# A hybrid attention and HGRN2 block on one core: the tensor engine's order written down in the source, with small products moved to common places

## The chip, the core and the metric

The program runs on one core of a Trainium2 chip. TensorE (PE) does the matrix products, VectorE (DVE) and ScalarE (ACT) the elementwise work, GpSimd (POOL) masks and powers, and SyncE (SP) issues the DMAs. Each engine works through its own list of instructions in order and stops at an instruction whose semaphores have not come. The metric is the device time of one execution, in microseconds (us).

## The reference

A block of a decoder for 512 positions of 1024 channels, in float32. One projection of the normalized input gives all branches; sliding-window attention with sinks and a gated linear recurrence (HGRN2) run in parallel, are merged by gates, and a SwiGLU layer follows.

```python
u = rmsnorm(h, norm_mix_g[layer])
p = jnp.einsum('bsd,de->bse', u, w_in[layer]) + b_in[layer]
aq, ak, av, hq, hf, hi, hg, gate_a, gate_b = split_columns(p)
y_attn = sliding_window_sink_attention(aq, ak, av, attn_sinks[layer])   # 16 heads, blocks of 128
y_hgrn = hgrn2_branch(hq, hf, hi, hg, lb_all[layer], hgrn_norm_g[layer]) # 8 heads, see below
ya = jnp.einsum('bse,ed->bsd', y_attn, w_branch_attn[layer])
yb = jnp.einsum('bse,ed->bsd', y_hgrn, w_branch_hgrn[layer])
merged = jax.nn.sigmoid(gate_a) * ya + jax.nn.sigmoid(gate_b) * yb
h = h + jnp.einsum('bsd,de->bse', merged, w_out[layer])
...
S_t = diag(f_t) S_{t-1} + k_t^T v_t ;  o_t = q_t S_t          # HGRN2, worked out in chunks
o = o * lax.rsqrt(jnp.mean(o * o, axis=-1, keepdims=True) + EPS)
o = o * norm_g * jax.nn.sigmoid(hg)
```

## The kernel before

**Large products.** Every float32 product of the projections is made of three products of split numbers (a high part and the rest, in fp32r). A projection (`project`, `mm3`, L404 to L406) is 24 matmuls of 128x512 into one PSUM tile `ps_big`; the values of HGRN (`values_hgrn`, L420 to L422) are 96 matmuls of 128x256 into `ps_v`. Weights come by DMA into `raw`; ACT makes the high part `wh` (L120) and DVE the rest `wl` (L126), two projections ahead, into three buffers each.

**The stream.** `stream()` is a generator that runs the projections in turn: queries and the gate of attention (`ga`), then for each of four pairs of heads `p` the HGRN values, then the projections `hf`, `hq` and `hg` for the two heads of the pair, and last the eight products `ya` with `w_branch_attn`. It yields three times in a projection (after a third, after two thirds and at the end) and six times in the values of a pair. Each yield is a slot.

**What stands beside it.** A table `beside` says after which slot each small step is called. An attention step `s` (group of four heads `s // 4`, block of queries `s % 4`) has three: `scores` (8 matmuls into `sc`, then the softmax on POOL, ACT and DVE, which ends with the multiplication of L507), `probs` (4 transposes into `pt`, L514; then ACT and DVE split the result and POOL masks it, L525 and L529) and `outputs` (2 or 4 matmuls into `pv`, L546). A head of HGRN has `hgrn_log` (ACT's Ln), `hgrn_prep` (a scan, exponentials and some thirteen operations on DVE, L629 to L658), `hgrn_intra` (matmuls into `pa` and `pc`), `hgrn_keys` (3 transposes `pk`), `hgrn_states` (`pu`), `hgrn_outputs` (matmuls into `po`, L705 and L707; then ACT squares them into `sq`, DVE sums, L713, and scales, L299, POOL takes the power, L300, and DVE writes the normalized `sq`, L715) and `hgrn_gate` (4 transposes of that `sq` into `pot`, L721, and DVE's product with the gate, L722). A pair's `hgrn_log` and `hgrn_prep` are called while the values of the next pair run (for the last pair: while the first `ya` runs).

**PSUM.** Small products share one tag of three buffers (`s1`); `sc` has a single buffer, and the large products have three.

**Who sets the order.** The program is recorded in the order of the calls, and a scheduler then places each engine's instructions by times that it estimates itself. So on PE the table only says about where a small product goes: the scheduler moves it behind further large products until its operands are due by the estimate. Later in the kernel, in the last part of the SwiGLU layer, a stretch is already under `tc.manual_schedule`, in which the named engines keep the order of the source.

Of the kernel before, what the change touches and what calls it, by code (L numbers as in the profile page):

```python
# [157 lines left out]
def block_kernel(ctx: ExitStack, tc: tile.TileContext, x, norm_mix_g, w_in, b_in,  # L158
# [153 lines left out]
    def transposed(half):  # L312
        xs = [ps1([P, 2, 256], "xs") for _ in range(3)] + [ps2([P, 4, 256], "xs")]
        views = [xs[j % 4][:, j // 4, :] for j in range(KD)]
        for t2 in range(2):
            t = 2 * half + t2
            if half == 0:
                normalize(t)
            for j in range(KD):
                pe.transpose(views[j][:, t2 * P:t2 * P + P], xt[:, t, j * P:(j + 1) * P],  # L320
                             ident)
        return views, xs[3][:, 2, 0:90]
# [19 lines left out]
    views, _ = transposed(0)  # L342
# [82 lines left out]
    def project(evac, ah=uh, al=ul):  # L425
        wh, wl = W.get()
        ps = psb([P, S], "ps_big")
        yield from mm3(ps, wh, wl, ah, al)
        evac(ps)
        yield  # L430
# [29 lines left out]
    def evac_q(c):  # L460
        def go(ps):
            bq = bias(c)
            for par in range(2):
                q = ap.tile([P, S], F32R, tag="q", bufs=8, name="qst")
                rs = slice(par * 64, par * 64 + 64)
                ot = slice(64 - par * 64, 128 - par * 64)
                act(q[rs], ps[rs], AF.Identity, bias=bq[rs])
                stt(q[ot], ps[rs], bq[rs], q.bitcast(F32)[rs], ALU.add, ALU.subtract)
                qsts[c // 64 + par] = q
        return go  # L470

    def evac_ga(j):
        def go(ps):
            act(m1[:, j, :], ps, AF.Identity, bias=bias(C_GA + P * j))
        return go
# [130 lines left out]
    def values_hgrn(p):  # L606
        wa, wb = W.get(), W.get()
        v = vals[p] = T("v", (P, NT, 256), 2, h1)
        for tp in range(2):
            ps = psb([P, 2, 256], "ps_v")  # L610
            for t2 in range(2):
                t = 2 * tp + t2
                mm3n(ps[:, t2, :], uh, ul, t, *wa, 0, True, False)
                yield
                mm3n(ps[:, t2, :], uh, ul, t, *wb, 4, False, True)
                tt(v[:, t, :], ps[:, t2, :], hib[:, 256 * p:256 * p + 256], ALU.add)
                if t2:
                    yield
# [107 lines left out]
    def evac_ya(j):  # L726
        def go(ps):
            tt(m1[:, j, :], ps, m1[:, j, :], ALU.mult)
        return go

    def stream():
        evac_q(0)(psq0)
        for i in range(4):
            for a in range(2):
                if i or a:
                    yield from project(evac_q(256 * i + P * a))
            if i:
                for a in range(2):
                    yield from project(evac_ga(2 * i - 2 + a))
        for a in range(2):  # L740
            yield from project(evac_ga(6 + a))
        for p in range(4):
            yield from values_hgrn(p)
            for ev in (evac_f, evac_hq, evac_hg):
                for a in range(2):
                    yield from project(ev(2 * p + a))
        for j in range(KD):
            yield from project(evac_ya(j), yh, yl)

    beside = {}  # L750

    def at(slot, f, *args):
        beside.setdefault(slot, []).append((f, args))
# [1 line left out]
    at(0, values)  # L755
    at(3, lower_bounds)
    for s in range(16):
        g0 = 3 * (1 + s)
        at(g0, scores, s // 4, s % 4)
        at(g0 + 4, probs, s // 4, s % 4)  # L760
        at(g0 + 8, outputs, s // 4, s % 4)
    at(3 * (1 + 15) + 8, open_hgrn)
    for p in range(4):
        g0 = 3 * (15 + 8 * p) + 24
        for a in range(2):
            hd = 2 * p + a
            at(g0, hgrn_log, hd)
            at(g0 + 2 * a + 1, hgrn_prep, hd)
            o = g0 + 8 + 9 * a
            for dt, f in ((0, hgrn_intra), (1, hgrn_keys), (3, hgrn_states),  # L770
                          (6, hgrn_outputs), (10, hgrn_gate)):
                at(o + dt, f, hd)
    slot = 0
    for _ in stream():
        for f, args in beside.pop(slot, ()):
            f(*args)
        slot += 1
    for s in sorted(beside):
        for f, args in beside[s]:
            f(*args)  # L780
    pools["h"].release()
    h1.release()
    h0.release()
# [227 lines left out]
    for kind, p in ffn[:-2]:  # L1011
# [5 lines left out]
        engines={mybir.EngineType.DVE, mybir.EngineType.Activation, mybir.EngineType.PE}))  # L1017
# [205 lines left out]
```

## Time and profile before

| | |
|---|---|
| median of 3 runs (lowest, highest) | 896.04 us (895.97, 896.45) |
| profiled execution | 895.81 us |
| its span, first to last instruction | 894.1 us |
| outside the span | 1.7 us |
| PE busy | 882.6 us, 99% of the span |
| DVE, ACT, POOL busy | 551.3, 397.0 and 155.1 us |
| the stretch that the change touches | about 31 to 425 us of the span |

In the rows of the profile, "L404 PE MATMUL ps_big<-uh,wh" is line 404, its engine and operation, and the tile written, an arrow and the tiles read; buffer numbers are left out. A row of the timeline has the start and the duration in us, and merges neighbours of one kind: x4 is four instructions as the chip ran them. A product of full float32 operands (`pa`, `pc`, `pu`, `po`) runs as two matmuls, so that its rows count double. Matmuls overlap: one of 128x512 is shown with 0.39 us, and the next starts 0.227 us after it.

### The profile page before, as it was taken

How to read it: one execution, taken by the hardware profiler on the slowest of the kernel's cores; microseconds unless marked ns; L12 is line 12 of the kernel's file. 1: busy time of each engine (PE TensorE's matmuls, PEld its weight loads, DVE VectorE, ACT ScalarE, POOL GpSimd, SP SyncE). 2: the span in 40 equal slices, each digit the busy share in tenths (PEclk: the TensorE clock that was granted, in tenths of full speed). 3: DMA queues.
4: the chain of work that ended last, by engine and by line, in shares of the span. 5: the costliest groups of instructions: out<-in, count | busy, mean ns of one | idle time of the engine just before them, and what ended most of it. 6: DMA issues, size and time to landing. Idle time of an engine off the chain costs nothing.

```text
span 894.1 us, 11244 instructions
## 1 busy us (share of the span) xinstructions
PE 882.6 (99%) x4410; PEld 746.8 (84%) x4410; DVE 551.3 (62%) x838; ACT 397.0 (44%) x637; POOL 155.1 (17%) x150
## 2 busy tenths in 40 slices
PE   8999999999999999999999999999999999999996
PEld 7988889888898988888888887888888888888785
DVE  5577877647494664844434345755655666566885
ACT  6566776646372544315223234332333333333454
POOL 3004434300000000000000002422133332122006
PEclk9999999999999999999999999999999999999999
DMA  8321211223213132221235232333343443435642
GB/s 261 95 95 48 95 48 48 95 95 95 95 28 114 48 115 74 94 81 62 94 96 189 93 95 89 107 134 113 122 141 96 141 127 108 135 101 174 252 163 95
DMA packets 74643, 97.26 MB, mean 109 GB/s; under 512 B 2043, under 2 KB 64605, under 8 KB 74589
## 3 DMA queue, kind: packets, MB, share of 16 engines
q1 hardware_dynamic: 74428, 96.27, 32.9%
q8 instruction: 35, 0.57, 0.3%
q10 hardware_dynamic: 160, 0.27, 0.1%
q14 instruction: 20, 0.16, 0.0%
HBM read 94.43 MB, written 2.10 MB: 108 GB/s over the span
## 4 chain that ended last, share of the span: by engine, by line
PE 96%; SPq 1%; DVE 1%; ACT 1%; POOL 0%; issue 0%; DMA 0%; DVEq 0%; POOLq 0%; ACTq 0%
PE ps_big L404 13%; PE ps_big L405 13%; PE ps_big L406 13%; PE ps_f L405 9%; PE ps_f L406 9%; PE ps_f L404 9%; PE s3y L989 3%; PE a22y L989 3%; PE s2y L989 3%; PE ps_v L421 2%; PE ps_v L422 2%; PE ps_v L420 2%; PE ps_o L421 2%; PE ps_o L422 2%; PE ps_o L420 2%; PE pv L546 1%
## 5 line engine op out<-in xcount | busy, mean ns | idle before, releaser
L120 ACT ACTIVATE wh<-raw 128x1024 fp32r<-128x1024 f32 (+1 forms) x168 | 172.3, 1031 | 344.4 <-PE ps_f L405 137.4
L126 DVE TENSOR_TENSOR wl<-raw,wh 128x1024 fp32r<-128x1024 f32 (+1 forms) x168 | 208.5, 1244 | 113.9 <-ACT wh L120 112.9
L404 PE MATMUL ps_big<-uh,wh 128*128 128x512 f32 x376 | 148.8, 396 | 0.0
L405 PE MATMUL ps_big<-ul,wh 128*128 128x512 f32 x376 | 147.8, 393 | 0.0
L406 PE MATMUL ps_big<-uh,wl 128*128 128x512 f32 x376 | 147.7, 393 | 0.0
L405 PE MATMUL ps_f<-u2l,wh 128*128 128x512 f32 x352 | 137.4, 390 | 0.0
L404 PE MATMUL ps_f<-u2h,wh 128*128 128x512 f32 x352 | 137.0, 390 | 0.2 <-ACT u2h L171 0.2
L406 PE MATMUL ps_f<-u2h,wl 128*128 128x512 f32 x352 | 137.0, 389 | 0.0
L406 PEld LDWEIGHTS ps_big<-uh,wl 128*128 128x128 f32 x376 | 70.7, 188 | 14.2
L405 PEld LDWEIGHTS ps_big<-ul,wh 128*128 128x128 f32 x376 | 70.8, 188 | 13.6
L404 PEld LDWEIGHTS ps_big<-uh,wh 128*128 128x128 f32 x376 | 70.7, 188 | 13.6
L405 PEld LDWEIGHTS ps_f<-u2l,wh 128*128 128x128 f32 x352 | 66.1, 188 | 14.0 <-issue 0.2
L404 PEld LDWEIGHTS ps_f<-u2h,wh 128*128 128x128 f32 x352 | 66.0, 188 | 14.0 <-ACT u2h L171 0.5
L406 PEld LDWEIGHTS ps_f<-u2h,wl 128*128 128x128 f32 x352 | 66.1, 188 | 13.9 <-issue 0.2
L954 POOL TENSOR_TENSOR zg<-zg,sgf 128x512 f32<-128x512 f32 x22 | 39.5, 1795 | 190.8 <-ACT sgf L176 190.8
L300 POOL TENSOR_TENSOR r<-ss,neghalf 128x4 f32<-128x4 f32 x8 | 10.1, 1262 | 232.8 <-DVE ss L299 232.8
L138 DVE TENSOR_TENSOR raw<-raw 128x512 f32<-128x512 f32 x44 | 31.7, 723 | 29.0 <-DMA raw<-in_w_ffn_down_dram 28.7
L951 DVE TENSOR_TENSOR zg<-ps_f,R 128x512 f32<-128x512 f32 x22 | 15.1, 691 | 38.0 <-PE ps_f L406 38.0
L955 POOL TENSOR_TENSOR zg<-zg,R 128x512 f32<-128x512 f32 x22 | 37.1, 1686 | 1.7
L420 PE MATMUL ps_v<-wh,uh 128*128 128x256 f32 x128 | 36.5, 285 | 0.0
L421 PE MATMUL ps_v<-wl,uh 128*128 128x256 f32 x128 | 36.3, 284 | 0.0
L422 PE MATMUL ps_v<-wh,ul 128*128 128x256 f32 x128 | 36.2, 284 | 0.0
(328 smaller groups left out, 1609.6 us busy)
## 6 DMA issues: line engine op xcount, KB each, us to landing
raw<-in_w_in_dram SPq DMA_DIRECT2D x27, 1024.0 KB, 5.2
raw<-in_w_ffn_gate_dram SPq DMA_DIRECT2D x11, 1024.0 KB, 5.2
raw<-in_w_ffn_up_dram SPq DMA_DIRECT2D x11, 1024.0 KB, 5.1
raw<-in_w_ffn_down_dram SPq DMA_DIRECT2D x11, 1024.0 KB, 4.8
raw<-in_w_ffn_down_dram SPq DMA_DIRECT2D x22, 512.0 KB, 4.5
raw<-in_w_branch_attn_dram SPq DMA_DIRECT2D x4, 1024.0 KB, 5.5
raw<-in_w_branch_hgrn_dram SPq DMA_DIRECT2D x4, 1024.0 KB, 4.8
raw<-in_w_out_dram SPq DMA_DIRECT2D x4, 1024.0 KB, 7.3
```

What stands on the lines that cost most here:

```text
L120: nc.scalar.activation(hv, src, AF.Copy)
L126: (low or nc.vector).tensor_tensor(lv, src, hv.bitcast(F32), ALU.subtract)
L138: add = lambda o, i0, i1: self.nc.vector.tensor_tensor(o, i0, i1, ALU.add)
L404: pe.matmul(ps, wh[:, k, :], ah[:, k, :], start=k == 0, stop=False)
L405: pe.matmul(ps, wh[:, k, :], al[:, k, :], start=False, stop=False)
L406: return raw_ins(pe.matmul(ps, wl[:, k, :], ah[:, k, :], start=False, stop=k == KD - 1))
L420: pe.matmul(ps, ah[:, k0 + k, ts], wh[:, k, :], start=first and k == 0, stop=False)
L421: pe.matmul(ps, ah[:, k0 + k, ts], wl[:, k, :], start=False, stop=False)
L422: pe.matmul(ps, al[:, k0 + k, ts], wh[:, k, :], start=False, stop=last and k == nk - 1)
L954: pool_e.tensor_tensor(zg, zg, sg, ALU.mult)
L955: pool_e.tensor_tensor(zg, zg, R, ALU.mult)
L989: pe.matmul(ps[i], x[:, ts], w, start=first and n == 0, stop=last and n == 2)
```

## The change

Three things change, all in the table and in the loop that works it off. First, the steps of attention move: `scores` of step s from slot 3 + 3s to slot 4 + 3s, `probs` from 4 to 6 slots behind `scores`, `outputs` from 8 to 12 slots behind. With these distances `outputs` of step s - 2, `probs` of step s and `scores` of step s + 2 fall on one slot. Second, in HGRN `hgrn_keys` moves from 1 slot behind `hgrn_intra` to the same slot, and `hgrn_gate` from 10 to 9 slots behind it, which for the first head of a pair is the slot of `hgrn_intra` and `hgrn_keys` of the second. Third, the loop runs under `tc.manual_schedule` for PE: PE keeps the order of the calls, while ACT, DVE, POOL and the DMAs are placed by the scheduler as before.

```diff
     for s in range(16):
-        g0 = 3 * (1 + s)
+        g0 = 4 + 3 * s
         at(g0, scores, s // 4, s % 4)
-        at(g0 + 4, probs, s // 4, s % 4)
-        at(g0 + 8, outputs, s // 4, s % 4)
-    at(3 * (1 + 15) + 8, open_hgrn)
+        at(g0 + 6, probs, s // 4, s % 4)
+        at(g0 + 12, outputs, s // 4, s % 4)
+    at(4 + 3 * 15 + 12, open_hgrn)
...
-            for dt, f in ((0, hgrn_intra), (1, hgrn_keys), (3, hgrn_states),
-                          (6, hgrn_outputs), (10, hgrn_gate)):
+            for dt, f in ((0, hgrn_intra), (0, hgrn_keys), (3, hgrn_states),
+                          (6, hgrn_outputs), (9, hgrn_gate)):
                 at(o + dt, f, hd)
     slot = 0
-    for _ in stream():
-        for f, args in beside.pop(slot, ()):
-            f(*args)
-        slot += 1
-    for s in sorted(beside):
-        for f, args in beside[s]:
-            f(*args)
+    with tc.manual_schedule(engines={mybir.EngineType.PE}):
+        for _ in stream():
+            for f, args in beside.pop(slot, ()):
+                f(*args)
+            slot += 1
+        for s in sorted(beside):
+            for f, args in beside[s]:
+                f(*args)
```

PE issues the same products before and after. Counted in its list from the first small product beside the stream to the last `hgrn_gate`, small products stand at 85 places between large ones before, and at 49 after. What follows is the order of instructions of the built programs; no time is in it.

The first place is on PE, in attention, where `ps_big` (projections) gives way to `ps_v` (the first HGRN values). Before:

```order
L489 MATMUL sc<-khh_430,qst 128x128
L490 MATMUL sc<-kll_432,qst 128x128
L405 MATMUL ps_big<-ul,wh_1370 128x512
...
L514 MATMUL pt<-ident,st 128x128 x4
L405 MATMUL ps_big<-ul,wh_1370 128x512
...
L420 MATMUL ps_v<-wh_1451,uh 128x256
L546 MATMUL pv<-ch,vhl_434 128x512
L421 MATMUL ps_v<-wl_1452,uh 128x256
L489 MATMUL sc<-khh_430,qst 128x256
L546 MATMUL pv<-cl,vhl_434 128x512
```

After:

```order
L406 MATMUL ps_big<-uh,wl_1337 128x512
L546 MATMUL pv<-ch,vhl_434 128x512
L546 MATMUL pv<-cl,vhl_434 128x512
...
L514 MATMUL pt<-ident,st 128x128 x4
L489 MATMUL sc<-khh_430,qst 128x256
L490 MATMUL sc<-kll_432,qst 128x256
...
L404 MATMUL ps_big<-uh,wh_1336 128x512
```

What stood at three places, partly mixed with large products, stands together: `pv` of one step, `pt` of a second and `sc` of a third.

The second place is on PE at the end of a pair's projections, where the second head's `po` is followed by the next values. Before:

```order
L406 MATMUL ps_big<-uh,wl_2375 128x512
L705 MATMUL po<-v,aT_1929 128x128 x2
L420 MATMUL ps_v<-wh_2419,uh 128x256
...
L707 MATMUL po<-st,lf 128x128
...
L422 MATMUL ps_v<-wh_2471,ul 128x256
L404 MATMUL ps_big<-uh,wh_2521 128x512
...
L420 MATMUL ps_v<-wh_2419,uh 128x256
...
L721 MATMUL pot<-ident,sq 128x128 x4
L420 MATMUL ps_v<-wh_2419,uh 128x256
```

After:

```order
L406 MATMUL ps_big<-uh,wl_2377 128x512
L705 MATMUL po<-v,aT_1988 128x128 x2
L707 MATMUL po<-st,lf 128x128
...
L420 MATMUL ps_v<-wh_2433,uh 128x256
...
L422 MATMUL ps_v<-wh_2473,ul 128x256
L721 MATMUL pot<-ident,sq 128x128 x4
L420 MATMUL ps_v<-wh_2433,uh 128x256
```

Between the end of `po` and `pot` stood 72 matmuls of `ps_v` (8 of them inside `po`) and 19 of `ps_big`; now 48 of `ps_v` stand there. The same holds at the end of the next pair. At the end of the third pair it was 73 of `ps_big` behind the last `po`, and is now 24.

The third place is on DVE at the same end of a pair: the operations of the next pair's `hgrn_prep`, among which the second head's sum (L713) and normalization (L715) stand. `E`, `K` and `QE` are tiles of `hgrn_prep`. Before:

```order
L629 SCALAR_TENSOR_TENSOR lf<-reset,lf 128x512 x2
L632 TENSOR_TENSOR d<-lf 128x512
L634 TENSOR_TENSOR e<-lf 128x512
L713 TENSOR_REDUCE ss_2513<-sq 128x4
...
L299 TENSOR_SCALAR ss_2513<-ss_2513 128x4
...
L656 TENSOR_TENSOR QE_2588<-q,lf 128x256
L616 TENSOR_TENSOR v<-ps_v,hib 128x256
L715 TENSOR_TENSOR sq<-po,r_2514 128x512
L646 TENSOR_TENSOR E_2632<-q,E_2632 128x512
```

After:

```order
L629 SCALAR_TENSOR_TENSOR lf<-reset,lf 128x512 x2
L632 TENSOR_TENSOR d<-lf 128x512
L634 TENSOR_TENSOR e<-lf 128x512
L713 TENSOR_REDUCE ss_2515<-sq 128x4
...
L299 TENSOR_SCALAR ss_2515<-ss_2515 128x4
...
L656 TENSOR_TENSOR QE_2590<-q,lf 128x256
L715 TENSOR_TENSOR sq<-po,r_2516 128x512
L646 TENSOR_TENSOR E_2634<-q,E_2634 128x512
```

DVE's list is the same down to L656; only one evacuation of values (L616) now stands behind L715 instead of before it. At the end of the third pair L715 now follows L656 and one `wl` (L126); before, eight more operations of `hgrn_prep` stood between.

## The prediction

> **What bounds the kernel now.** I read the page's busy line first, then PE's waits.
>
> ```profile
> PE 882.6 (99%) x4410; PEld 746.8 (84%) x4410; DVE 551.3 (62%) x838; ACT 397.0 (44%) x637; POOL 155.1 (17%) x150
> PE pg L293 <- POOL ident masks.py:199: 1.9, 1, 1.9
> ...
> PE s3y L989 <- DVE y1l L983: 0.2, 1, 0.2
> ```
>
> PE is busy for 99% of the span. Six lines of waits, of which the first and last stand here, come to 3.8 us together, and none lies in the stretch that the change touches. So before the change no small product there keeps PE waiting. Two things can alter the time: how densely PE's products follow each other, and new waits on PE, which count in full since nothing else is the bound.
>
> How dense they are shows in starts on the timeline. First comes undisturbed work near the end, then large products behind four transposes in attention:
>
> ```profile
> 884.09 0.39 PE L1119 MATMUL a22y<-wh,zl 128*128 128x512 f32 x1
> ...
> 886.13 0.39 PE L1119 MATMUL s2y<-wh,zl 128*128 128x512 f32 x1
> 122.53 0.60 PE L514 MATMUL pt<-ident,st 128*128 128x128 f32 x4
> 122.88 0.48 PE L406 MATMUL ps_big<-uh,wl 128*128 128x512 f32 x1
> 123.19 0.40 PE L404 MATMUL ps_big<-uh,wh 128*128 128x512 f32 x1
> ...
> 125.51 0.40 PE L546 MATMUL pv<-ph,vhl 128*128 128x512 f32 x1
> ```
>
> Undisturbed, nine products take 2.04 us, 0.227 each. Behind the transposes, the ten from 123.19 to 125.51 take 2.32 us where 2.27 would do. An interruption thus costs about 0.05 us.
>
> **Gathering.** Small products stand at 49 places instead of 85, so 36 interruptions go: 36 x 0.05 = 1.8 us gained. The bounds are 0 (a larger group disturbs as much as the small ones did) and 3.6 us (each costs double); I take the row's 1.8.
>
> **The order of the source.** The scheduler could put further large products ahead of a small one; now PE stops where the table says. Each kind of place needs the moment its operands are ready, measured from an event that the change leaves alone.
>
> *Second head's gate.* At the end of a pair's projections PE issues `po`, then 48 `ps_v`, then `pot`, which reads the `sq` that L715 writes. These rows of three timelines (ACT, then DVE and POOL) run from the end of the second pair's projections in the old kernel, where the first pair's second head is at its gate:
>
> ```profile
> 244.85 1.06 ACT L120 ACTIVATE wh<-raw 128x1024 fp32r<-128x1024 f32 x1 [3.99 <-PE ps_big L405]
> 249.37 0.58 ACT L171 ACTIVATE sq<-po 128x512 f32<-128x512 f32 x1
> 248.97 2.34 DVE L629 TENSOR_TENSOR_SCAN lf<-reset,lf 128x512 f32<-128x512 f32 x2 [1.80 <-ACT lf L176]
> 252.41 0.68 DVE L713 TENSOR_REDUCE ss<-sq 128x4 f32<-128x512 f32 x1
> 254.78 2.05 POOL L300 TENSOR_TENSOR r<-ss,neghalf 128x4 f32<-128x4 f32 x1 [25.84 <-DVE ss L299]
> 256.75 0.42 DVE L656 TENSOR_TENSOR QE<-q,lf 128x256 f32<-128x256 f32 x1
> 257.42 0.68 DVE L715 TENSOR_TENSOR sq<-po,r 128x512 f32<-128x512 f32 x1
> ```
>
> ACT works in a fixed order: `wh`, two sigmoids, a table load, Ln twice, and only then the square of `po`. DVE's sum (L713) stands behind two scans and two subtractions, and its normalization (L715) behind ten more operations, the last of them L656. An earlier `po` hurries none of it. PE's side:
>
> ```profile
> 224.03 0.61 PE L705 MATMUL po<-v,aT 128*128 128x128 f32 x4
> ...
> 225.74 0.48 PE L405 MATMUL ps_big<-ul,wh 128*128 128x512 f32 x1
> 244.89 0.61 PE L705 MATMUL po<-v,aT 128*128 128x128 f32 x4
> 245.45 0.28 PE L421 MATMUL ps_v<-wl,uh 128*128 128x256 f32 x1
> 245.57 0.28 PE L422 MATMUL ps_v<-wh,ul 128*128 128x256 f32 x1
> ```
>
> A whole `po` takes 225.74 - 224.03 us, less one `ps_big` that ran within it (0.31, as from 122.88 to 123.19 above): 1.40. Values follow every 0.12 us: 48 x 0.12 = 5.76, and I allow 0.1 for the interruption. On the old clock PE would stand at `pot` at 244.89 + 1.40 + 5.86 = 252.15. L715 no longer has L616 ahead of it: it can begin once L656 ends, near 257.1 (POOL's power is done at 256.8), and end at 257.8. PE waits 5.65 us. Behind `pot` on PE stand 48 values, which nothing else holds up, and the rest of the stream. The next pair's end, in the same order:
>
> ```profile
> 298.01 0.27 PE L705 MATMUL po<-v,aT 128*128 128x128 f32 x1
> 309.87 0.41 DVE L656 TENSOR_TENSOR QE<-q,lf 128x256 f32<-128x256 f32 x1
> ```
>
> Arrival 298.01 + 7.26 = 305.27; L715 begins near 310.2 and ends near 310.9: 5.65 us. At the third pair's end the first `ya`, 24 x 0.227 = 5.44 us and the 0.1, stands between:
>
> ```profile
> 351.14 0.61 PE L705 MATMUL po<-v,aT 128*128 128x128 f32 x4
> 363.60 1.22 DVE L126 TENSOR_TENSOR wl<-raw,wh 128x1024 fp32r<-128x1024 f32 x1
> ```
>
> Arrival 351.14 + 1.40 + 5.54 = 358.1; L715 now comes right behind this `wl`, which ends at 364.8, and takes 0.68, to 365.4 with some overlap: 7.3 us. The fourth pair's last gate keeps 35 large products ahead of it, as before. Sum: 5.65 + 5.65 + 7.3 = 18.6 us. The new lists of ACT and DVE hold these chains as the old ones do; a microsecond each way per wait, 3 in all, bounds what a different mix may do.
>
> *First head's gate.* `pot` comes 24 large products behind `po` instead of 32 and `pa`, `pc`:
>
> ```profile
> 228.97 0.69 DVE L715 TENSOR_TENSOR sq<-po,r 128x512 f32<-128x512 f32 x1 [1.20 <-POOL r L300]
> 400.06 0.75 DVE L722 SCALAR_TENSOR_TENSOR of<-pot,prm,sg 128x512 f32<-128x512 f32 x1 [1.07 <-PE pot L721]
> 371.14 0.60 PE L721 MATMUL pot<-ident,sq 128*128 128x128 f32 x4
> 372.83 0.47 PE L404 MATMUL ps_big<-yh,wh 128*128 128x512 f32 x1
> ```
>
> L715 ends 229.66 - 224.03 = 5.6 us behind the start of `po`; PE arrives at 1.40 + 5.54 = 6.9. No wait. `pot`, `pa` and `pc` now take the three small PSUM buffers in turn, and `pk` right behind them needs that of `pot`, which L722 empties. L722 starts when `pot` is through, 0.6 us after its start, and ends 1.4 us after it. `pot`, `pa` and `pc` take PE 1.69 (371.14 to 372.83), which hides it. In the fourth pair a 512-wide operation on `ya` stands before L722 on DVE, such as take 0.69 to 0.75 here, of which 0.3 are covered: 0.4 us, once. Ends: 0 and 4 x 0.4.
>
> *Attention.* One of the longest softmaxes, from its first product to its last operation:
>
> ```profile
> 118.81 0.28 PE L489 MATMUL sc<-khh,qst 128*128 128x256 f32 x1
> ...
> 128.07 0.77 DVE L507 TENSOR_TENSOR st<-st,sm 128x512 f32<-128x512 f32 x1
> ```
>
> From the first `sc` to the end of L507 it is 10.0 us. Six slots are 48 large products, 10.9 us, even without the small ones between: no wait. POOL, which masks between `pt` and `pv`, has the same six slots and is busy for 17% of the span. No step that moves issues a DMA; SP's loads go on waiting for the buffers that PE frees.
>
> **The clock.** PE has not stood still like this in the old kernel, except at the ends. By stretches (span, PE busy and count first; behind POOL's the granted clock):
>
> ```profile
> 1.86:6.03 4.17, 4.17 (x20) 4.17 (x21) 0.05 (x1) 2.00 (x3) 0.45 (x2) 1.00 0.97 313
> 6.03:10.00 3.97, 3.27 (x27) 2.73 (x25) 2.63 (x5) 3.01 (x5) 1.11 (x2) 1.00 1.12 387
> 886.50:890.08 3.58, 0.01 (x1) 0.00 (x0) 2.56 (x6) 2.02 (x6) 3.04 (x4) 1.00 0.19 73
> 890.08:894.10 4.02, 0.00 (x0) 0.00 (x0) 0.24 (x1) 0.22 (x1) 0.00 (x0) 0.50 0.51 198
> ```
>
> 3.6 us after PE's last product the clock falls to half. At the start, PE needs 4.17 us for 20 small products, 0.21 each, and afterwards 3.27 for 27, 0.12 each: a cold start loses 4.17 - 20 x 0.12 = 1.8 us. All three waits are longer than 3.6 us, so I add 3 x 1.8 = 5.3. Ends: 0 (it never falls) and twice that.
>
> [...]
>
> **Sum.** 895.8 - 1.8 + 18.6 + 0.4 + 5.3 = 918.3 for the profiled execution; the median lies 0.2 higher: 918.5 us.
>
> **Rivals.**
>
> *The clock holds.* One fall, seen at the end, may need more than a wait on PE gives. Then 918.5 - 5.3 = 913.2. Chance 0.22.
>
> *The gates do not wait.* If L713 and L715 in fact come free before PE arrives, only the gathering is left: 918.5 - 18.6 - 0.4 - 5.3 = 894.2, not slower. It decides on whether L715 ends within 7.2 us of the end of the projections; in the old rows that is 13.2, and DVE's new list still has L656 ahead of it. Chance 0.06, half of it beyond 0.2%.
>
> *Softmax comes late too.* Gathered places hand ACT and DVE three results at once; if that stretches the chain from 10.0 us to one microsecond more than the 12.7 that lie between (48 large products and eight `pv`, 56 x 0.227), at each of 14 steps, it is 918.5 + 14 = 932.5. DVE's 62% on the page and the 2.7 us in hand speak against it. Chance 0.08.
>
> **Numbers.** The forecast has 0.64. Low: the clock holds and each wait is a microsecond shorter, 913.2 - 3 = 910. High: cold phases cost double, and the waits add 2: 918.5 + 5.3 + 2 = 926. That takes in two cases and leaves out 0.14. Against 0.2% (1.8 us, about what a measurement of this kernel can tell from no change): faster 0.03, same 0.03, slower 0.94.
>
> **What would show it.** Right: PE's waits name DVE's `sq` (L715) before `pot` about 18.6 us in three places, the granted clock dips behind them, and large products follow more evenly. Wrong: PE waits at `pt`, `pv` or `sc`, or has no wait before `pot`, or the clock stays at 1.00.

## The result and the profile after

The changed kernel takes 929.01 us (median of 4 runs, 928.14 to 931.2) against 896.06 us before (895.97 to 896.45): a ratio of 1.0372, with a 95% interval of 1.036 to 1.0384. The direction of the forecast is right; the time lies 3 us above its range. The profiled execution took 929.77 us, 928.1 of it the span: 34.0 more than before.

The page's busy line of the changed kernel, and the first two of PE's waits (total us, times, longest):

```profile
PE 890.7 (96%) x4410; PEld 753.4 (81%) x4410; DVE 549.4 (59%) x838; ACT 397.7 (43%) x637; POOL 144.3 (16%) x150
PE ps_v L420 <- DVE v L616: 18.1, 8, 4.6
PE pot L721 <- DVE sq L715: 7.2, 1, 7.2
```

Two things are new. PE waits, as forecast, but only once at `pot`; most of it, 18.1 us, is at L420, the first product of a block of HGRN's values, where the forecast had no wait. And PE is busy 8.1 us longer with the same 4410 products.

To see where, I cut both traces at the same places in PE's work: the first value of the second, third and fourth pair, and the first L420 product behind the stream (into `ps_o`). Columns: window, length, then busy us of PE, PEld, DVE, ACT, POOL, the granted clock. Before, then after:

```profile
30.00:193.67 163.67, 163.67 (x866) 139.68 (x864) 115.62 (x187) 102.25 (x237) 45.84 (x67) 1.00 0.25 80
193.67:245.25 51.58, 51.58 (x306) 45.46 (x304) 31.41 (x58) 25.35 (x35) 1.02 (x1) 1.00 0.29 92
245.25:298.38 53.13, 53.13 (x322) 47.09 (x320) 32.98 (x62) 25.47 (x36) 3.06 (x2) 1.00 0.25 79
298.38:492.82 194.44, 194.44 (x989) 165.37 (x988) 107.53 (x173) 76.68 (x102) 6.01 (x5) 1.00 0.29 95
```

```profile
30.00:195.20 165.20, 164.17 (x867) 140.02 (x867) 113.78 (x188) 102.84 (x237) 34.11 (x67) 1.00 0.25 80
195.20:257.20 62.00, 55.72 (x316) 49.35 (x314) 31.72 (x59) 26.61 (x36) 1.01 (x1) 0.94 0.24 77
257.20:317.50 60.30, 54.81 (x321) 48.54 (x320) 32.93 (x63) 25.57 (x36) 3.10 (x2) 0.97 0.22 70
317.50:526.80 209.30, 196.87 (x979) 167.16 (x978) 107.33 (x173) 75.76 (x101) 6.97 (x5) 0.98 0.27 88
```

Attention, the first row, is 1.5 us longer; the three HGRN rows are 10.4, 7.2 and 14.9 us longer. Idle PE (length less busy) is 1.0 + 6.3 + 5.5 + 12.4 = 25.2 us, where before had none; PE's busy time rises by 0.5 + 4.1 + 1.7 + 2.4 = 8.8 us, all but the first 0.5 in the rows whose clock is under 1.00. (The page's 8.1 is less because PE is busy 0.7 us less before these windows begin.) Together 34.0; the rest of the span is as long as before.

The wait at L420 is best seen on DVE's and PE's timelines at the end of the second pair's projections, the place that the forecast worked out in detail. DVE first, then PE:

```profile
259.80 2.34 DVE L629 TENSOR_TENSOR_SCAN lf<-reset,lf 128x512 f32<-128x512 f32 x2 [1.80 <-ACT lf L176]
...
263.24 0.68 DVE L713 TENSOR_REDUCE ss<-sq 128x4 f32<-128x512 f32 x1
...
264.44 0.42 DVE L616 TENSOR_TENSOR v<-ps_v,hib 128x256 f32<-128x256 f32 x1
...
267.57 0.42 DVE L656 TENSOR_TENSOR QE<-q,lf 128x256 f32<-128x256 f32 x1
267.90 0.69 DVE L715 TENSOR_TENSOR sq<-po,r 128x512 f32<-128x512 f32 x1
```

```profile
260.03 0.28 PE L422 MATMUL ps_v<-wh,ul 128*128 128x256 f32 x1
264.91 0.58 PE L420 MATMUL ps_v<-wh,uh 128*128 128x256 f32 x1 [4.60 <-DVE v L616]
...
269.15 0.60 PE L721 MATMUL pot<-ident,sq 128*128 128x128 f32 x4
```

The four blocks `t` of a pair's values lie two to a PSUM tile. PE has done block 0 at 260.3 and stands until DVE has read it out (L616, over at 264.9), because block 1 writes the same tile. DVE is late with L616 for the reason that the forecast gives for L713 and L715: it stands behind the scans. When PE then reaches `pot`, at 269.15, `sq` has been there since 268.6. So one wait has taken the other's place.

L616 is no earlier before. There it runs 8.4 us behind the first value (after: 7.2), but PE has other work (DVE, then PE):

```profile
253.61 0.42 DVE L616 TENSOR_TENSOR v<-ps_v,hib 128x256 f32<-128x256 f32 x1
```

```profile
252.20 0.40 PE L404 MATMUL ps_big<-uh,wh 128*128 128x512 f32 x1
...
256.31 0.39 PE L404 MATMUL ps_big<-uh,wh 128*128 128x512 f32 x1
256.53 0.28 PE L420 MATMUL ps_v<-wh,uh 128*128 128x256 f32 x1
```

From 252.20 to 256.5 PE works at the next projection. The order of the built programs shows how (tile numbers, large products in a row; "waits for DVE" stands where the first of them has a semaphore to wait for that DVE sets behind L616):

```
before:  ps_v_2530 24 | ps_v_2608 24 | ps_big 19 | ps_v_2530 24 (waits for DVE) | pot | ps_v_2608 24 | ps_big 5
after:   ps_v_2532 24 | ps_v_2532 24 (waits for DVE) | pot | ps_v_2616 24 | ps_v_2616 24 (waits for DVE) | ps_big 24
```

The scheduler had turned the blocks to 0, 2, 1, 3 and put 19 products of a projection between the halves of a tile. That is nowhere in the source, and keeping PE to the source undid it.

### The profile page after: what moved, and what is told of

Read it like the earlier page. It is cut to its first block, busy times and chain, and to the rows that moved or that the text cites. A ratio compares the mean times of both kernels' runs of the same rounds, so it can differ in the third digit from the quotient of the medians.

```text
span 928.1 us, 11221 instructions
## 1 busy us (share of the span) xinstructions
PE 890.7 (96%) x4410; PEld 753.4 (81%) x4410; DVE 549.4 (59%) x838; ACT 397.7 (43%) x637; POOL 144.3 (16%) x150
## 4 chain that ended last, share of the span: by engine, by line
PE 88%; DVE 6%; ACT 3%; SPq 1%; issue 1%; POOL 0%; DMA 0%; DVEq 0%; POOLq 0%; ACTq 0%
PE ps_big L404 12%; PE ps_big L405 12%; PE ps_big L406 12%; PE ps_f L405 9%; PE ps_f L406 9%; PE ps_f L404 9%; PE s3y L990 3%; PE a22y L990 3%; PE s2y L990 3%; PE ps_o L420 2%; PE ps_o L422 2%; PE ps_o L421 2%; PE pv L546 1%; PE a11b L990 1%; DVE lf L629 1%; PE ps_v L420 1%
## 5 line engine op out<-in xcount | busy, mean ns | idle before, releaser
L126 DVE TENSOR_TENSOR wl<-raw,wh 128x1024 fp32r<-128x1024 f32 (+1 forms) x168 | 208.1, 1242 | 108.9 <-ACT wh L120 108.8
L420 PE MATMUL ps_v<-wh,uh 128*128 128x256 f32 x128 | 39.8, 311 | 18.1 <-DVE v L616 18.1
L420 PEld LDWEIGHTS ps_v<-wh,uh 128*128 128x128 f32 x128 | 26.9, 210 | 19.8 <-DVE v L616 19.7
L421 PE MATMUL ps_v<-wl,uh 128*128 128x256 f32 x128 | 38.5, 301 | 0.0
L422 PE MATMUL ps_v<-wh,ul 128*128 128x256 f32 x128 | 38.4, 300 | 0.0
```

The costliest lines, as they stand in the source:

```text
L126: (low or nc.vector).tensor_tensor(lv, src, hv.bitcast(F32), ALU.subtract)
L420: pe.matmul(ps, ah[:, k0 + k, ts], wh[:, k, :], start=first and k == 0, stop=False)
L421: pe.matmul(ps, ah[:, k0 + k, ts], wl[:, k, :], start=False, stop=False)
L422: pe.matmul(ps, al[:, k0 + k, ts], wh[:, k, :], start=False, stop=last and k == nk - 1)
```

## The experiments

**own_tiles: a PSUM tile for each block of values.**

```diff
-            ps = psb([P, 2, 256], "ps_v")
             for t2 in range(2):
+                ps = psb([P, 256], "ps_v")
                 t = 2 * tp + t2
-                mm3n(ps[:, t2, :], uh, ul, t, *wa, 0, True, False)
+                mm3n(ps, uh, ul, t, *wa, 0, True, False)
...
-                tt(v[:, t, :], ps[:, t2, :], hib[:, 256 * p:256 * p + 256], ALU.add)
+                tt(v[:, t, :], ps, hib[:, 256 * p:256 * p + 256], ALU.add)
```

> The changed kernel, but each of the four blocks of values gets a PSUM tile of its own, so that the first product of a block no longer has to come behind DVE's evacuation (L616) of the block before it. Theory A, the shared tile: the 18.1 us of waits at L420 go, and the forecast's two waits at pot, which these had swallowed, come back: pot waits for L715 at the ends of pairs 1, 2 and 3 by 5.65, 5.65 and 7.2 us, 18.5 in all; with three falls of the clock at about 1.8 us that is 896.0 + 18.5 + 5.3 less at most 0.6 for the gathering: 919 to 920 us, 9 to 10 below the changed kernel. Theory B, a late DVE: L616 is only where DVE's delay shows; PE then stops as long at the next tile that DVE or ACT has not freed, waits stay at 25 us and the time at 927 to 930 us.

Measured: 920.01 us, ratio 1.0269 (1.0255 to 1.0283). PE's wait, then DVE and PE at the second pair's end:

```profile
PE pot L721 <- DVE sq L715: 18.7, 3, 7.2
```

```profile
257.13 0.68 DVE L715 TENSOR_TENSOR sq<-po,r 128x512 f32<-128x512 f32 x1
```

```profile
257.87 1.12 PE L721 MATMUL pot<-ident,sq 128*128 128x128 f32 x4 [5.79 <-DVE sq L715]
```

Theory A. No wait is left at L420, and the forecast's three waits stand where it put them: 18.7 us against 18.6, L715 over at 257.8 as worked out. With values that nothing holds up the forecast's kernel exists, and takes 920.0 where 918.5 was forecast.

**paired: the tiles as they were, the blocks in the order 0, 2, 1, 3.**

```diff
-        for tp in range(2):
-            ps = psb([P, 2, 256], "ps_v")
-            for t2 in range(2):
+        two = [psb([P, 2, 256], "ps_v") for _ in range(2)]
+        for t2 in range(2):
+            for tp in range(2):
+                ps = two[tp]
...
-                if t2:
+                if tp:
```

> The changed kernel with its PSUM tiles for the values as they are, but the four blocks in the order 0, 2, 1, 3, so that the two halves of a tile are never worked on one behind the other: PE still keeps the order of the source, which is now written as the scheduler had ordered the blocks by itself. Theory, the shared tile: 24 products of 128x256 (2.9 us) now stand between a block and the other half of its tile; L420's waits of 2.7 and 3.6 us fall to below 1, those of 4.6 to 1.7, and pot waits for the rest as in the kernel with own tiles, 5.8, 5.8 and 7.2 us less what L420 waited before it: 920 to 922 us. Rival: the DVE evacuation is not what holds L420, and its waits stay at 18 us, the time at 929.

Measured: 921.3 us, 1.0283 (1.0266 to 1.0301). PE's waits (the edit moves the lines by one):

```profile
PE pot L722 <- DVE sq L716: 18.7, 3, 7.2
```

These are the waits of own_tiles, by another edit: the shared tile again. L420 never waits long enough to be in the list, and even the 1.7 us that were expected are not there. The expectation had the order of PE's work wrong: `pot` stands between blocks 2 and 1, and its wait for L716 (252.42 to 258.21 us at the second pair's end) outlasts the evacuation that block 1 needs (over at 254.1).

**late_gate: only the second head's gate later.** 14 slots behind `hgrn_intra` instead of 9.

```diff
-                          (6, hgrn_outputs), (9, hgrn_gate)):
+                          (6, hgrn_outputs), (9 + 5 * a, hgrn_gate)):
```

> The changed kernel, but the second head's gate comes 14 slots behind its hgrn_intra instead of 9 (for the first head 9 as in the changed kernel). Theory A: pot's wait of 7.2 us at the end of pair 3 goes with its fall of the clock (1.7 us); the eight waits at L420 stay at 18.1 us: 929.0 - 7.2 - 1.7 = 920.1 us. Theory B, a late DVE: the wait moves to whatever reads DVE's next results, and the time stays within 2 us of 929.

Measured: 921.64 us, 1.0291 (1.0275 to 1.0307).

```profile
PE ps_v L420 <- DVE v L616: 15.0, 8, 4.6
...
PE pk L684 <- DVE of L722: 1.6, 1, 1.6
```

The wait at `pot` is gone and does not come back elsewhere in its size, so theory B, that PE pays for a late DVE wherever it is, falls. A small new one shows at `pk`, which needs the PSUM buffer of `pot`. The expectation kept L420 at 18.1 us; of the 3.1 us that are missing, 2.7 are at one place, the second wait behind the first pair's projections (changed kernel, then late_gate):

```profile
210.54 0.58 PE L420 MATMUL ps_v<-wh,uh 128*128 128x256 f32 x1 [3.58 <-DVE v L616]
```

```profile
210.57 0.39 PE L420 MATMUL ps_v<-wh,uh 128*128 128x256 f32 x1 [0.90 <-DVE v L616]
```

L616 is over at the same time in both. In late_gate PE arrives 2.7 us later, because here the wait before halved the clock (its windows are in the last section), and so it waits that much less: here, where another engine ends the next wait, the slow clock cost next to nothing. In the profiled execution (919.94 us, the fastest of four, up to 923.2) the waits are 25.3 - 16.6 = 8.7 us shorter, and PE works 13.2 us at half clock instead of 15.7, which saves 1.3: together 10.0, where its span is 9.9 us shorter. Why the median lies 1.7 us above that execution, no trace shows.

**own_late: both edits together.**

> Both edits together: a PSUM tile for each block of values, and the second head's gate 14 slots behind. Theory A: no wait of more than 0.5 us is left in the stream, the clock stays at 1.00, and what is left against the kernel before is the gathering alone: 896.0 - 1.8 = 894.2 us by the forecast's 0.05 us for an interruption, 895.4 us by what is left over in the changed kernel's trace (0.6 us). Theory B, a late DVE: PE stops at pa or at the next projection's tile instead, 10 us or more, and the time is above 906 us.

Measured: 899.69 us, 1.004 (1.0028 to 1.0053), above the 894.2 to 895.4 of theory A and far below theory B. Of 33 us 3.7 are left, and one kind of wait in the stream:

```profile
PE pk L684 <- DVE of L722: 3.7, 3, 1.6
```

The late gate now puts `pot` 6 products ahead of `pa`, `pc` and `pk`, and three small buffers make `pk` wait for L722, which follows a block of `hgrn_prep` on DVE. It is the mechanism that the forecast priced at 0.4 us, at places that only the late gate makes.

**no_waits: own_late, with the first head's keys one slot later again.**

```diff
-            for dt, f in ((0, hgrn_intra), (0, hgrn_keys), (3, hgrn_states),
+            for dt, f in ((0, hgrn_intra), (1 - a, hgrn_keys), (3, hgrn_states),
```

> As the kernel with both edits (own PSUM tiles, second head's gate 14 slots behind), but the first head's hgrn_keys stands one slot behind its hgrn_intra again, as in the old table. In the kernel with both edits pk waited three times, 3.7 us in all, for DVE's L722 to free the small PSUM buffer of pot. If that is all that is left, the three waits go, none above 0.5 us stays in the stream, and the time is 899.7 - 3.7 = 896.0 us: the gathering is worth nothing that can be told from no change. If gathering is worth the forecast's 1.8 us it must come out at 894.2 or below. If PE instead meets another late buffer, pu or po, the time stays at 899 to 900.

Measured: 895.55 us (median of 11 runs) against 895.90, ratio 0.9993, 0.9985 to 1.0002: no difference that can be told from none. No wait is left in the stream, as expected. So the whole loss of the change was waits on PE and what came with them, and the gathering itself brings next to nothing. By window, from the first projection to the second pair's values, and on to the end of the stream (no_waits, the old kernel):

```profile
32.12:194.18 162.06, 162.06 (x854) 138.38 (x853) 112.26 (x184) 101.15 (x235) 34.10 (x67) 1.00 0.25 79
194.18:493.19 299.01, 299.01 (x1609) 258.11 (x1608) 170.66 (x293) 127.51 (x171) 11.04 (x8) 1.00 0.28 92
```

```profile
31.33:193.67 162.34, 162.34 (x855) 138.35 (x853) 114.35 (x184) 100.94 (x236) 45.84 (x67) 1.00 0.25 78
193.67:492.82 299.15, 299.15 (x1609) 257.92 (x1608) 171.92 (x293) 127.51 (x171) 10.09 (x8) 1.00 0.28 92
```

0.28 us in attention and 0.14 in HGRN, with PE never idle in any of the four.

**own_late_spread: own_late, with attention's small products scattered again.**

```diff
-        at(g0 + 6, probs, s // 4, s % 4)
-        at(g0 + 12, outputs, s // 4, s % 4)
-    at(4 + 3 * 15 + 12, open_hgrn)
+        at(g0 + 7, probs, s // 4, s % 4)
+        at(g0 + 14, outputs, s // 4, s % 4)
+    at(4 + 3 * 15 + 14, open_hgrn)
```

> As the kernel with both edits, but with attention's small products scattered again: probs 7 and outputs 14 slots behind scores instead of 6 and 12, so that the three kinds fall on three different slots: some 48 places in attention instead of some 18, PE still in the order of the source. If an interruption costs 0.05 us as the forecast had it, 30 more of them cost 1.5 us over the kernel with both edits. If the gathering is worth only what the changed kernel's trace leaves for it, 0.2 us or less. Softmax has seven slots, so no wait at pt is expected either way.

Measured: 900.24 us, 1.0047 (1.0035 to 1.006), against 899.69; the intervals overlap, so the times alone do not separate them. The attention stretch of the traces does, own_late_spread first, then own_late:

```profile
31.50:194.30 162.80, 162.80 (x854) 138.29 (x853) 111.97 (x184) 100.65 (x236) 35.25 (x67) 1.00 0.25 78
```

```profile
31.42:193.49 162.07, 162.07 (x855) 138.29 (x853) 112.28 (x184) 101.25 (x235) 34.22 (x67) 1.00 0.25 79
```

0.73 us for some 30 places: about 0.024 us each, half of the forecast's 0.05, and between the two expectations. It is one trace each, but the stretch repeats well: own_tiles, paired, no_waits and fill_own, whose attention is that of own_late, take 162.05 to 162.06 us for it.

**fill: unread products on PE in front of five waits of the changed kernel.** `fill(n, a, b)` issues n products into a small PSUM tile.

```diff
+                if t2:
+                    n = {(1, 0): 20, (1, 1): 28, (2, 0): 36, (3, 0): 36}.get((p, tp), 0)
+                    fill(n, uh[:, 0, 0:P], wb[0][:, 0, :])
                 mm3n(ps[:, t2, :], uh, ul, t, *wa, 0, True, False)
...
+        if hd == 5:
+            fill(28, yh[:, 0, 0:P], yh[:, 0, :])
         pt = ps1([P, NT, P], "pot")
```

> The changed kernel, with products that nobody reads put on PE in front of five of its waits: 20 and 28 of 128x256 at the two blocks of values behind pair 1, 36 of 128x256 at the first such block behind pairs 2 and 3 (0.12 us each), 28 of 128x512 before pot at the end of pair 3 (0.227 each), each set some 0.4 to 1 us shorter than the wait in the changed kernel. What PE has to wait for comes no earlier and no later. Theory, the clock is a cost of its own: in the changed kernel PE worked 16.35 us at half clock behind the waits, which loses 8.2 us; if PE is kept busy the clock stays at 1.00 and the time falls by about 8 us, to 921, though there is more work. Rival, the waits alone make the difference: the time stays at 929 or rises by what the fillers overrun.

Measured: 926.69 us, 1.0344 (1.033 to 1.0358). The clock stays at 1.00 through the stream (0.998 over the span, as in the old kernel), but only 2.3 us come back. One premise did not hold. With the products in, DVE's list is another, presumably because they change the scheduler's estimates: a value's evacuation (here L625) stands three or four operations later. PE's waits, the products aside:

```profile
PE ps_v L420 <- DVE v L625: 5.9, 8, 1.3
PE pot L732 <- DVE sq L724: 2.0, 3, 0.8
```

Unread products (120 x 0.12 + 28 x 0.227 = 20.8 us) and waits (7.9) make 28.7 us, 3.4 more than the 25.3 of waits in the changed kernel. So the run does not size the clock, and another was made.

**fill_own: the same in own_tiles.** 44 unread products of 128x256 in front of `pot` for the second heads of the first two pairs, 28 of 128x512 for that of the third.

```diff
+        if hd in (1, 3):
+            fill(44, uh[:, 0, 0:P], uh[:, 0, 0:256])
+        if hd == 5:
+            fill(28, yh[:, 0, 0:P], yh[:, 0, :])
         pt = ps1([P, NT, P], "pot")
```

> The kernel with a PSUM tile for each block of values, whose only waits are three at pot (5.8, 5.8 and 7.2 us), with products that nobody reads in front of pot: 44 of 128x256 (5.3 us) at the ends of pairs 1 and 2, 28 of 128x512 (6.4 us) at the end of pair 3. DVE's list is the same with and without them, instruction for instruction, and nothing after pot waits, so that a slower clock behind it is paid in full. Behind its three waits that kernel's trace shows PE at half clock for 3.2, 4.2 and 3.7 us. Theory, the forecast's term for the clock is right in size: with PE kept busy the clock stays at 1.00 and the time falls by half of 11.1, 5.5 us, from 920.0 to 914.5. Rival, the half clock costs little or the fillers cost their own time: 919 us or more.

Measured: 914.59 us, 1.0208 (1.0192 to 1.0223): 5.4 us less than own_tiles, with more work on PE, whose clock stays at 1.00 through the stream. What is left of the waits, and, from own_tiles, the stretches at half clock that it saves:

```profile
PE pot L731 <- DVE sq L721: 1.8, 3, 0.8
```

```profile
257.87:261.10 3.23, 3.23 (x15) 3.23 (x16) 3.23 (x10) 0.03 (x1) 0.00 (x0) 0.50 0.00 0
318.36:322.54 4.18, 4.18 (x20) 4.18 (x21) 4.18 (x13) 0.03 (x1) 0.00 (x0) 0.50 0.00 0
380.32:383.98 3.66, 3.66 (x11) 3.08 (x12) 3.66 (x11) 0.00 (x0) 0.00 (x0) 0.50 0.82 285
```

Half of 11.07 us is 5.5. The price of the clock is shown by itself, and the forecast's 5.3 for three falls was right.

**table_only and manual_only: the halves of the change.** The first is the new table in the old loop, the second the old table in the new loop.

> The changed table alone, with the scheduler placing PE's instructions as before. Theory: the waits come from PE keeping the order of the source, so with the scheduler free they are gone: 896 us, within 1.5. Rival: the new places themselves are bad, and several microseconds of waits at pot, pk or L420 stay: 905 us or more.

> The old table with PE keeping the order of the source. Theory: the waits at L420 for L616 are there as in the changed kernel (18 us), pot stands 60 values behind po and waits little, and in attention pt follows scores after 32 large products (7.3 us) and some 1.9 us of small ones against a softmax of 10 us, so that it waits up to 0.8 us at each of 16 steps: 925 to 940 us. Rival: without the new distances attention becomes the larger loss, 2 to 3 us at each step: 960 us or more. Were it at 896, the new table and not the order of the source would be the cost.

Measured: table_only 900.82 us, 1.0059 (1.0045 to 1.0073); manual_only 932.53 us, 1.0417 (1.0401 to 1.0433). Of each, the waits that matter:

```profile
PE ps_big L404 <- ACT sgm L176: 2.7, 1, 2.7
```

```profile
PE ps_v L420 <- DVE v L616: 16.4, 8, 4.6
PE pot L721 <- DVE sq L715: 5.2, 1, 5.2
...
PE sc L489 <- DVE qst L468: 1.6, 2, 1.1
```

The order of the source alone costs the whole loss and a little more; it, not the new table, is the main cause. Both expectations missed a part. The scheduler does not undo the new table entirely: two waits for ACT, this and one of 1.6 us, stand behind the fourth pair, and the time lies between the two expectations; why PE's list comes out so there stays open. And in manual_only `pot`, expected to wait little, waits 5.2 us behind the fourth pair's projections, and no `pt` waits, though the old table leaves only four slots for the softmax: its attention waits at `sc` instead.

## Why the prediction was wrong

- **Where the loss lies: half right.** It named PE's waits at the second heads' gates of the first three pairs, behind DVE operations that the next pair's scans delay, and a fall of the clock behind each. Those places, that engine and that delay are what the traces show.
- **The step that failed** is "Behind `pot` on PE stand 48 values, which nothing else holds up", and with it "Values follow every 0.12 us: 48 x 0.12 = 5.76". A value's block waits for L616 of the block that shares its PSUM tile. In the changed kernel that holds PE for 4.6 us ahead of `pot` at the ends of the second and the third pair's projections (so that the two waits of 5.65 us never come about), and behind the first pair's projections, where no gate stands and the forecast had nothing, for 2.7 + 3.6 us. With the second blocks and the first pair's values that makes 18.1 us at L420; only the third wait at `pot` is left, 7.2 us where 7.3 was worked out. Sum 25.3 instead of 18.6 + 0.4.
- A block waits for the read-out of another one's columns: the two blocks take 256 columns each of one tile, and PE's 4.60 us end with DVE's read of the other half; own_tiles and paired take the wait away by parting the two. Why reads and writes of different columns of a tile are put in order, no run here shows.
- The row that tells was in the old trace: L616 at 253.61, 1.2 us behind L713. It was not asked why PE could afford that. own_tiles shows that everything else in this term was right, to 0.1 us in 18.7.
- **The clock**: that each long wait costs clock as well was right; the size was 7.9 instead of 5.3, because there were four falls and one was long. The condition was not right: the forecast had a fall need 3.6 us without a product, and one of the four came with a wait of 3.58 us, in late_gate one with a wait of 2.70 (see the last section). At half clock PE worked in these windows of the changed kernel:

```profile
210.54:216.59 6.05, 6.05 (x26) 5.94 (x27) 4.21 (x11) 1.54 (x2) 0.00 (x0) 0.50 0.00 0
264.91:267.78 2.87, 2.87 (x13) 2.87 (x14) 2.87 (x8) 0.99 (x3) 2.09 (x1) 0.50 0.00 0
325.81:329.22 3.41, 3.41 (x19) 3.41 (x18) 3.41 (x9) 2.08 (x4) 1.97 (x1) 0.50 0.01 2
390.67:394.08 3.41, 3.41 (x10) 2.89 (x11) 3.41 (x11) 0.00 (x0) 0.00 (x0) 0.50 0.82 285
```

  Half of 15.74 us is 7.9 (the expectation for fill had 16.35 for it, having counted the third from PE's start at 325.22). Where three falls had to be paid, in own_tiles, the forecast's number was met, 1.6, 2.1 and 1.8 us against 1.8 each. The 1.8 had been worked out from the spacing of small products at the start, in a row whose clock reads 1.00.
- **The gathering**: 0.4 us instead of 1.8. Ten products behind one group of transposes were too small a sample; own_late_spread gives half of the row's 0.05 us. The forecast's end of 0, that a larger group disturbs as much, is nearer to what was measured than the 1.8 it took; that this is the reason is not shown.
- **`pk`**: no wait in the changed kernel; the 0.4 was not needed, and the three small buffers bit only once the gate was moved.
- **Attention, the first head's gate, POOL**: no wait at `pt`, `pv`, `sc`, `pa` or at a first head's `pot`, as forecast. PE's list of waits names none.
- **The rivals**: the clock did not hold, the gates did wait, softmax was not late. Of the signs named beforehand, "18.6 us in three places" before `pot` failed in the changed kernel and the dips of the clock came.

Of the 10.5 us between 918.5 and 929.0 the waits make 6.3, the clock 2.6 and the gathering 1.4. Added up from the old kernel: 25.2 us of idle PE, 7.9 for the clock, and 0.9 that is left of 34.0. Part of that is the first product behind each of nine waits: PE's shown busy time is 0.28 us where it counts 0.12 in a row, 9 x 0.16 = 1.4, less the 0.4 of the gathering. This last split is argued, not shown.

## What to carry to other kernels

A scheduler that one turns off may have been hiding waits that are nowhere in the source: before freezing an engine's order, list what it had moved, block by block and with buffer numbers, and ask of every late operation on another engine why nobody waited for it. Here two accumulations that share a PSUM tile are in effect one buffer, and in source order the second waits for the first one's read-out, 4.6 us at the longest; a tile each, or another order of the blocks, removes that (no wait at L420 in the lists of own_tiles and paired). A wait on PE of some microseconds can cost more than its length, and the price of it (1.6 to 2.1 us each in own_tiles) can be measured by itself by giving PE something to do; where another engine ends the next wait, as in late_gate, that wait swallows it: PE came 2.7 us later to L616's result and waited that much less.

## What the hardware showed

The clock fell behind a wait of 2.70 us, too. The first wait behind pair 1 is 2.70 us long in the changed kernel and in late_gate alike, and ends at 200.95 and 200.99 us. In the changed kernel nothing followed; in late_gate the clock halved. In the changed kernel the half-speed stretches shown above end at 216.59, 267.78, 329.22 and 394.08: 15, 18 and 19 times 3.413 us apart. Windows of that grid and of late_gate's own, the changed kernel's first:

```profile
199.52:202.93 3.41, 1.98 (x16) 1.98 (x17) 3.41 (x5) 0.56 (x2) 0.00 (x0) 1.00 0.02 5
```

```profile
196.88:200.29 3.41, 1.40 (x12) 1.20 (x10) 1.61 (x2) 2.98 (x5) 0.00 (x0) 1.00 0.00 1
200.29:203.70 3.41, 2.71 (x12) 2.72 (x13) 3.41 (x6) 0.98 (x1) 0.00 (x0) 0.50 0.03 5
```

In the one the wait lies across a boundary and PE is busy for 1.98 us of the window; in the other for 1.40 of 3.41, and the next window is at half speed. So in these two runs the same wait cost clock or did not by where it fell on the grid.

The half-speed stretches of three other traces lie on such grids as well: in late_gate they start at 200.29, 261.73 and 319.76, 18 and 17 times 3.413 us apart; in own_tiles they end at 261.10, 322.54 and 383.98, 18 times each; two of manual_only start at 42.09 and 205.93, 48 times. Of the windows at full clock just ahead of these starts, PE was busy for 1.40, 0.00 and 1.43 us in late_gate and for 1.06 us in the one of manual_only that ends at 205.93. Here are a window of the changed kernel that was not followed by half clock, and then the other of manual_only, which was, with the window behind it:

```profile
318.98:322.40 3.42, 1.65 (x14) 1.44 (x13) 2.29 (x3) 3.38 (x5) 0.00 (x0) 1.00 0.00 0
```

```profile
38.67:42.09 3.42, 1.77 (x12) 1.38 (x11) 2.34 (x3) 0.84 (x2) 0.00 (x0) 1.00 0.04 13
42.09:45.50 3.41, 3.41 (x10) 2.74 (x10) 1.60 (x3) 1.37 (x7) 0.00 (x0) 0.50 0.00 0
```

The first is followed by a window at 1.00 (322.40 to 325.81). So PE's busy time in the profile does not sort the windows by itself: 1.65 us was followed by full clock, 1.77 by half. In table_only a stretch of 3.41 us in which PE was busy for 1.16 us was followed by full clock, too; whether it is a window of a grid there is not shown:

```profile
420.72:424.13 3.41, 1.16 (x11) 0.96 (x9) 1.99 (x3) 3.10 (x4) 0.30 (x1) 1.00 0.03 10
424.13:427.55 3.42, 2.99 (x13) 2.50 (x14) 0.69 (x1) 1.53 (x3) 0.71 (x1) 1.00 0.87 302
```

How much idle time in a window brings the clock down is thus not settled by these runs.

Where the waits fall on the grid may also be why kernels with long waits scatter more from run to run (928.14 to 931.2 for the change, 919.5 to 921.2 for own_tiles) than the same with PE kept busy (926.59 to 926.88 for fill, 914.27 to 915.01 for fill_own); no run tests that.

In own_tiles, too, the first fall (at 254.27) came 2.2 us into its wait of 5.79 us, which began at 252.08: earlier than the 3.6 us that the forecast had read at the end of the old trace.
